# One hybrid encoder layer: attention's order written out for every engine, and the convolutions' middle stage interleaved

## The chip, the cores and the metric

The kernel runs on one core of a Trainium2 chip. A core has five engines with an instruction queue each: TensorE (PE, the matmul array, with a queue of its own for loading weights, PEld), VectorE (DVE), ScalarE (ACT), GpSimd (POOL) and SyncE (SP), which here only issues DMAs. Every queue is worked in its order; semaphores make an instruction wait for other engines and for DMAs. PE reads from SBUF and writes into PSUM, eight banks of 512 f32 columns; DVE and ACT read PSUM. The metric is the device time of one execution in microseconds.

## The reference

A layer has a token-mixing half and an expert half. The change is in the token mixing, of which this is the core (2048 tokens, 8 heads, 512 convolved channels):

```python
q = (rms_norm(cq_raw, q_norm_g) @ w_qb)                 # 8 heads x (64 + 32 rotary)
kv = (rms_norm(c_kv, kv_norm_g) @ w_kvb)                # keys and values of 8 heads
s = einsum('bqhd,bkhd->bhqk', qn, k_nope) + einsum('bqhr,bkr->bhqk', qr, k_rope)
p = softmax(s * scale, axis=-1)
a = einsum('bhqk,bkhd->bqhd', p, v)
...
z = parts[0]                                            # the other group: two long convolutions
for o in range(2):
    y = irfft(rfft(z, n=2 * S, axis=1) * filt_f[:, o], n=2 * S, axis=1)[:, :S]
    z = parts[o + 1] * (y + z * hyena_bias[o])
mixed = concatenate([rms_norm(a), rms_norm(z)]) @ w_o
```

## The kernel before, in words

The stage of the change lies between the input projection and the output projection. It has two streams of work that share all engines.

**Attention** (`attention`, lines 771 to 897) goes over 32 blocks: 8 heads, each with four blocks of 512 queries. A block has 16 steps over 128 keys. In a step PE makes the scores in three matmuls (lines 866 to 868, operands split into a high and a low part), ACT takes the exponential twice (lines 874 and 875, once rounded to the high part), DVE subtracts to get the low part (line 876, recorded at the helper's line 65), POOL adds the high part to an accumulator for the row sums (line 881), and PE multiplies with the values two steps later (`pv`, lines 859 and 860). The maximum of every row is found ahead, one block early, by `max_step`: one matmul (line 803) and one DVE reduction (line 805), 16 to a block. `max_row` turns the maxima into one more row of the query operand: DVE reduces and copies (lines 810, 811), PE transposes (814), ACT writes the row (815), and the next block's first score matmul reads it. `query` makes the query operand two blocks ahead; `free_sums` and `close_block` take a finished block out of PSUM, divide and store it. PSUM holds three score banks, two for maxima and the like (`x`), one each for the two value products, and one (`h`) for the other stream.

**The convolutions** (`hyena`, lines 631 to 768) are FFTs written as matmuls, for two orders `o` and two halves `i` of the channels: `spectrum` transforms the filters (matmul at line 669), `fwd1` is the first stage of the input's transform (652), `first_half` its second stage and the product with the spectrum (matmul 691, DVE 695, ACT 697 and 698, POOL 704 and 706), `second_half` the inverse's first stage (716), `inv` its last with the gate (736, 739). First and second half are the middle stage. All stages pass their results through DRAM (`Ad`, `F_dr`, `Bd`, `Z1`, `HY`), with loads and stores on SP's queue. Keys and values of the other heads (`values`, `other_keys`) come first in the same stream.

The two streams are generators. `drive` advances attention by a step and the other stream by a share of a step (1.5 for the first 12, then 0.7), and drains it at the end. This is only the order in which the code is written: the planner (`schedule_with_timeline_sim`) simulates the program with durations of its own and puts each engine's instructions in the order in which they come up there. Behind the stage, the output projection (lines 970 and on) loads `w_o` in eight pieces, splits each into a high and a low part (lines 1018, 1025), loads rows of both streams, transposes and multiplies (lines 73 to 75). Its weights are loaded into SBUF that the convolutions had.

Of the kernel before, what the change touches and what calls it, by code (L numbers as in the profile page):

```python
# [25 lines left out]
NT = 16  # L26
# [22 lines left out]
def hybrid_layer(ctx, tc, I, out):  # L49
# [581 lines left out]
    def hyena(hp, hw, bk):  # L631
# [7 lines left out]

        def fwd1(o, i, q4):  # L640
            hc = slice(i * HC, (i + 1) * HC)
            w1c = hw.tile([128, 4, 256], F32, name="ta", bufs=3)
            SY.dma_start(w1c, I["k_w1c"][:, q4 * 1024:q4 * 1024 + 1024].rearrange("p (q m) -> p q m", q=4))
            zt = hw.tile([128, 4, HC], F32, name="tb")
            SY.dma_start(zt, ZS[o][:, q4 * 4:q4 * 4 + 4, hc])
            for q2 in range(2):
                ev = hw.tile([128, 2, 2, HC], F32, name="tc")
                for qq in range(2):
                    ql = q2 * 2 + qq
                    p = bk("h")  # L650
                    for mt in range(2):
                        T.matmul(p[:, mt * HC:(mt + 1) * HC], w1c[:, ql, mt * 128:mt * 128 + 128], zt[:, ql, :],
                                 start=True, stop=True)
                    A.activation(ev[:, :, qq, :], p.rearrange("p (m c) -> p m c", m=2), AF.Copy)
                    if qq == 0:
                        yield
                for mt in range(2):
                    q0 = q4 * 4 + q2 * 2
                    SY.dma_start(Ad[2 * o + i][mt * 128:mt * 128 + 128, q0:q0 + 2, :], ev[:, mt])
                yield  # L660

        def spectrum(o, g4):
            kt = hw.tile([128, 4, CH], F32, name="tc")
            SY.dma_start(kt, pat(Af[o], g4 * 4 * 128 * CH, [[CH, 128], [128 * CH, 4], [1, CH]]))
            for g2 in range(2):
                ev = hw.tile([128, 2, CH], F32, name="ta", bufs=3)
                for gg in range(2):
                    p = bk("h")
                    T.matmul(p, g2m[:, 1 if g4 + g2 + gg == 0 else 0, :], kt[:, g2 * 2 + gg, :], start=True, stop=True)  # L669
                    A.activation(ev[:, gg, :], p, AF.Copy)  # L670
                    if gg == 0:
                        yield
                g0 = g4 * 4 + g2 * 2
                SY.dma_start(F_dr[o][g0:g0 + 2].rearrange("g p c -> p g c"), ev)
                yield

        def first_half(o, i, g4):
            hc = slice(i * HC, (i + 1) * HC)
            kt = hw.tile([128, 4, HC], F32, name="ta", bufs=3)
            SY.dma_start(kt, pat(Ad[2 * o + i], g4 * 4 * 128 * HC, [[HC, 128], [128 * HC, 4], [1, HC]]))  # L680
            ff = hw.tile([128, 4, 2, HC], F32, name="tc")
            for hh in range(2):
                SY.dma_start(ff[hh * 64:hh * 64 + 64], pat(F_dr[o], g4 * 4 * 128 * CH + i * HC,
                                                           [[CH, 64], [128 * CH, 4], [64 * CH, 2], [1, HC]]))
            ys = YS[g4] = []
            for g2 in range(2):
                gs = slice(g2 * 2, g2 * 2 + 2)
                p = bk("h")
                for gg in range(2):
                    gi = g2 * 2 + gg  # L690
                    T.matmul(p[:, gg * HC:(gg + 1) * HC], zm[:, 2 if g4 + gi == 0 else 0, :], kt[:, gi, :],
                             start=True, stop=True)
                pv = p.rearrange("p (g c) -> p g c", g=2)
                pr = hw.tile([128, 2, HC], F32, name="pr")
                V.tensor_tensor(pr, pv, ff[:, gs, 0], OP.mult)
                zs = hw.tile([128, 2, HC], F32, name="zs")
                A.activation(zs[0:64], pv[64:128], AF.Copy, scale=-1.0)
                A.activation(zs[64:128], pv[0:64], AF.Copy)
                yield
                if g4 + g2 == 0:  # L700
                    p = bk("h")
                    T.matmul(p[:, 0:HC], zm[:, 3, :], kt[:, 0, :], start=True, stop=True)
                    A.activation(zs[:, 0], p[:, 0:HC], AF.Copy)
                G.tensor_tensor(zs, zs, ff[:, gs, 1], OP.mult)
                y = hw.tile([128, 2, HC], F32, name="y", bufs=4)
                G.tensor_tensor(y, pr, zs, OP.add)
                ys += [y[:, 0], y[:, 1]]

        def second_half(o, i, g4):
            bt = hw.tile([128, 4, HC], F32, name="tb")  # L710
            ys = YS.pop(g4)
            for g2 in range(2):
                pi = bk("h")
                for gg in range(2):
                    gi = g2 * 2 + gg
                    T.matmul(pi[:, gg * HC:(gg + 1) * HC], ivm[:, 1 if g4 == 0 and gi == 0 else 0, :], ys[gi],  # L716
                             start=True, stop=True)
                A.activation(bt[:, g2 * 2:g2 * 2 + 2, :], pi.rearrange("p (g c) -> p g c", g=2), AF.Copy)
                yield
            SY.dma_start(pat(Bd[2 * o + i], g4 * 4 * 128 * HC, [[HC, 128], [128 * HC, 4], [1, HC]]), bt)  # L720

        def inv(o, i, q4):
# [4 lines left out]
            gt = hw.tile([128, 4, HC], F32, name="tb")  # L727
            SY.dma_start(gt, HZ[1 + o][:, qs, hc])
            for q2 in range(2):
                b2 = hw.tile([128, 2, 2, HC], F32, name="tc")  # L730
                q0 = q4 * 4 + q2 * 2
                SY.dma_start(b2, Bd[2 * o + i][:, q0:q0 + 2, :].rearrange("(k p) q c -> p k q c", k=2))
                p = bk("h")
                for qq in range(2):
                    for kt in range(2):
                        T.matmul(p[:, qq * HC:(qq + 1) * HC], w2i[:, q2 * 2 + qq, kt, :], b2[:, kt, qq, :],
                                 start=kt == 0, stop=kt == 1)
                q_ = slice(q2 * 2, q2 * 2 + 2)
                V.tensor_tensor(gt[:, q_], p.rearrange("p (q c) -> p q c", q=2), gt[:, q_], OP.mult)
                if q2 == 0:  # L740
                    yield
            SY.dma_start(ZO[o][:, qs, hc], gt)

        YS = {}

        def turns(*gens):
            gens = list(gens)
            while gens:
                for g in list(gens):
                    if next(g, gens) is gens:  # L750
                        gens.remove(g)
                    else:
                        yield

        for o in range(2):
            for g4 in range(8):
                yield from spectrum(o, g4)
            for i in range(2):
                for q4 in range(4):
                    yield from fwd1(o, i, q4)  # L760
            for i in range(2):
                yield from first_half(o, i, 0)
                for g4 in range(1, 9):
                    yield from turns(second_half(o, i, g4 - 1), *([first_half(o, i, g4)] if g4 < 8 else []))
            for i in range(2):
                for q4 in range(4):
                    yield from inv(o, i, q4)
                    yield


    def attention(kp, aw, bk):
        mz = kp.tile([128, 4, 128], F32, name="mz")
# [34 lines left out]
        def max_row(n):  # L807
            qh, ql, mx = blk[n]
# [16 lines left out]
        def close_block(n, osb, acc):  # L825
# [4 lines left out]
            for i in range(4):  # L830
# [5 lines left out]
                            rc[:, :, None].to_broadcast([128, 4, 64]), OP.mult)  # L836
            (G if n == NB - 1 else SY).dma_start(AO[:, b * 4:b * 4 + 4, h * 64:h * 64 + 64], oo)
# [4 lines left out]
        for j in range(16):  # L842
            max_step(0, j)
            yield
        max_row(0)
        pend = osb = None
        for n in range(NB):
            h, b = divmod(n, 4)
            if b == 0 and 0 < h < H - 1:
                load_head(h + 1)  # L850
            qh, ql, _ = blk[n]
            kh, kl, vt = khs[h % 2][:, 0], khs[h % 2][:, 1], vts[h % 2]
            po, pl = bk("o"), bk("l")
            acc = aw.tile([128, 512], F32, name="acc")
            ph = {}

            def pv(k):
                eh, el = ph.pop(k)
                T.matmul(po, vt[:, k, 0:128], eh, start=k == 0, stop=k == NT - 1)  # L859
                T.matmul(pl[0:66], vt[:, k, 64:130], el, start=k == 0, stop=k == NT - 1)  # L860

            maxes = iter(range(16))
            for k in range(NT):
# [11 lines left out]
                A.activation(p, p, AF.Exp, scale=SCALE)  # L875
                lo_of(V, el, p, eh)
                ph[k] = eh, el
# [4 lines left out]
                if k == 1 and pend is not None:  # L882
                    osb = free_sums(*pend[1:])
                if k >= 2:
# [811 lines left out]
```

## Time and profile before

| | |
|---|---|
| time, median of 3 runs | 3461.23 us (3448.82 to 3462.97) |
| the profiled execution | 3456.35 us, span 3454.6 us |
| PE busy over the span | 3196.6 us (93%) |
| DVE, ACT, POOL busy | 2301.5, 1697.8, 1456.5 us |

Busy counts the instructions' own time, and matmuls overlap each other. [...] In the chain of waits each entry is the time by which that instruction moved the end on, so that matmuls following each other without a gap show their pace there.

### The profile page before, as it was taken

Reading aid. Unit: us, or ns where it says so; the run is one execution under the profiler, and the core shown is the slowest. Engines: PE = TensorE matmul, PEld = TensorE weight load, DVE = VectorE, ACT = ScalarE, POOL = GpSimd, SP = SyncE. Lnnn points to the kernel's source line nnn. Section 1 sums busy time; section 2 is a strip of 40 time slices with the busy share of each in tenths; the row PEclk is TensorE's granted clock in tenths of the full one; section 3 lists DMA queues with packets and bytes.
Section 4 is the critical chain, followed back from the end, with each engine's and each line's share of the span. In section 5 each row is a group of like instructions: output and inputs, shape, how many; then the busy total and the mean of one; then the engine's idle time right before and its main releaser. Section 6 shows DMA issues by size and latency. Waiting matters only on the chain.

```text
span 3454.6 us, 41964 instructions
## 1 busy us (share of the span) xinstructions
PE 3196.6 (93%) x14790; PEld 2477.7 (72%) x14790; DVE 2301.5 (67%) x3528; ACT 1697.8 (49%) x2569; POOL 1456.5 (42%) x1134
## 2 busy tenths in 40 slices
PE   7899999899989999999998699599999999999897
PEld 3667787666767776677776488477788877887676
DVE  7975343776677776667774377776656566565886
ACT  4762222566667664667774244233444344444442
POOL 5750000556678784658886266300100010000564
PEclk9999999699999999999999899799999999999998
DMA  6444353356466467647456643455666566665784
GB/s 192 158 150 118 111 145 94 97 175 175 156 162 150 108 160 236 176 165 163 119 126 194 222 155 131 150 171 186 215 199 203 183 217 210 208 203 186 268 279 160
DMA packets 373755, 594.16 MB, mean 172 GB/s; under 512 B 36859, under 2 KB 190013, under 8 KB 373097
## 3 DMA queue, kind: packets, MB, share of 16 engines
q1 hardware_dynamic: 347097, 528.95, 48.5%
q0 software_dynamic: 26304, 62.00, 7.1%
q8 instruction: 117, 1.92, 0.2%
q14 instruction: 93, 0.76, 0.1%
q10 hardware_dynamic: 144, 0.52, 0.0%
HBM read 438.84 MB, written 152.58 MB: 171 GB/s over the span
## 4 chain that ended last, share of the span: by engine, by line
PE 70%; DVE 11%; DMA 8%; issue 4%; POOL 3%; ACT 3%; SPq 0%; POOLq 0%; DVEq 0%; ACTq 0%
PE g L73 9%; PE g L74 9%; PE g L75 8%; PE s L866 3%; PE s L867 3%; PE s L868 3%; PE o L859 3%; PE l L860 3%; PE x L803 3%; PE mm L75 3%; PE mm L74 3%; PE mm L73 3%; DMA w<-in_w_ada_dram 3%; PE h L669 2%; PE h L716 1%
## 5 line engine op out<-in xcount | busy, mean ns | idle before, releaser
L881 POOL TENSOR_TENSOR acc<-acc,eh 128x512 f32<-128x512 f32 x480 | 615.8, 1283 | 157.3 <-ACT eh L874 132.3
L65 DVE TENSOR_TENSOR wl<-raw,wh 128x2048 fp32r<-128x2048 f32 (+1 forms) x210 | 473.3, 2256 | 225.0 <-ACT wh L59 224.0
L59 ACT ACTIVATE wh<-raw 128x2048 fp32r<-128x2048 f32 x192 | 367.5, 1915 | 439.9 <-PE g L75 341.4
L65 DVE TENSOR_TENSOR el<-s,eh 128x512 fp32r<-128x512 f32 x512 | 349.2, 687 | 158.2 <-ACT s L875 153.2
L805 DVE TENSOR_REDUCE mx<-x 128x1 f32<-128x512 f32 x512 | 346.4, 685 | 140.5 <-PE x L803 138.1
L73 PE MATMUL g<-wh,xh 128*128 128x512 f32 x1024 | 411.1, 402 | 3.2 <-DVE xh L62 2.3
L74 PE MATMUL g<-wl,xh 128*128 128x512 f32 x1024 | 408.3, 399 | 1.6 <-DVE wl L65 1.5
L75 PE MATMUL g<-wh,xl 128*128 128x512 f32 x1024 | 407.5, 398 | 1.0 <-DVE xl L65 1.0
L874 ACT ACTIVATE eh<-s 128x512 fp32r<-128x512 f32 x512 | 304.9, 596 | 205.1 <-PE s L868 179.0
L1495 POOL DMA_INDIRECT ACC<-ye,idx x30 | 65.8, 2195 | 691.0 <-DVE ye L1486 565.5
L875 ACT ACTIVATE s<-s 128x512 f32<-128x512 f32 x512 | 304.5, 595 | 0.0
L860 PE MATMUL l<-el,vt 128*66 128x512 f32 x512 | 226.5, 446 | 0.6 <-DVE acc L820 0.4
L73 PEld LDWEIGHTS g<-wh,xh 128*128 128x128 f32 x1024 | 193.0, 188 | 47.0 <-DVE xh L62 3.1
L74 PEld LDWEIGHTS g<-wl,xh 128*128 128x128 f32 x1024 | 193.1, 189 | 45.4 <-DVE wl L65 2.7
L75 PEld LDWEIGHTS g<-wh,xl 128*128 128x128 f32 x1024 | 192.7, 188 | 45.7 <-DVE xl L65 1.8
L803 PE MATMUL x<-kh,qt 96*128 96x512 f32 x512 | 221.9, 446 | 1.8 <-DVE mx L805 1.6
L866 PE MATMUL s<-qt,kh 97*128 97x512 f32 x512 | 214.9, 420 | 3.3 <-ACT qt L815 2.7
L73 PE MATMUL mm<-uT,wh 128*128 128x512 f32 x512 | 207.8, 407 | 5.4 <-DVE uT L62 5.4
L73 PE MATMUL g<-wh,hh 128*128 128x512 f32 x512 | 205.9, 403 | 5.8 <-ACT hh L59 5.8
L74 PE MATMUL g<-wl,hh 128*128 128x512 f32 x512 | 205.9, 402 | 5.2 <-DVE wl L65 5.2
L867 PE MATMUL s<-qt,kh 96*128 96x512 f32 x512 | 208.2, 407 | 0.0
L868 PE MATMUL s<-qt,kh 96*128 96x512 f32 x512 | 207.2, 405 | 0.0
(408 smaller groups left out, 6988.9 us busy)
## 6 DMA issues: line engine op xcount, KB each, us to landing
raw<-in_w_gate_dram SPq DMA_DIRECT2D x64, 1024.0 KB, 5.0
raw<-in_w_up_dram SPq DMA_DIRECT2D x64, 1024.0 KB, 7.1
raw<-in_w_down_dram SPq DMA_DIRECT2D x64, 1024.0 KB, 10.1
tc<-F_dr SPq DMA_DIRECT2D x64, 512.0 KB, 5.2
w<-in_w_ada_dram SPq DMA_DIRECT2D x48, 512.0 KB, 4.4
Af<-ev SPq DMA_DIRECT2D x32, 512.0 KB, 2.6
tc<-Af SPq DMA_DIRECT2D x16, 1024.0 KB, 6.4
F_dr<-ta SPq DMA_DIRECT2D x32, 512.0 KB, 3.0
```

The costliest lines, as they stand in the source:

```text
L59: return A.activation(hi, src, AF.Copy)
L65: return eng.tensor_tensor(lo, src, hi.bitcast(F32), OP.subtract)
L73: first = T.matmul(o, wh, xh, start=start, stop=False)
L74: T.matmul(o, wh, xl, start=False, stop=False)
L75: T.matmul(o, wl, xh, start=False, stop=stop)
L803: T.matmul(p, qh[0:96, i * 128:i * 128 + 128], khs[h % 2][0:96, 0, c * 512:c * 512 + 512], start=True, stop=True)
L805: V.tensor_reduce(mx[:, i, c:c + 1], p, axis=AX.X, op=OP.max)
L860: T.matmul(pl[0:66], vt[:, k, 64:130], el, start=k == 0, stop=k == NT - 1)
L866: T.matmul(p, kh[0:97, ks], qh[0:97, :], start=True, stop=False)
L867: T.matmul(p, kh[0:96, ks], ql[0:96, :], start=False, stop=False)
L868: T.matmul(p, kl[0:96, ks], qh[0:96, :], start=False, stop=True)
L881: G.tensor_tensor(acc, acc, eh.bitcast(F32), OP.add)
```

## The change

The convolutions: `first_half` and `second_half` become one task, `mid`, whose step `g4` also does the second half of step `g4 - 1`. Each task first issues its loads, then computes in four steps; a fixed list of tasks interleaves the middle stage of one half with other stages of the other half. A task's loads are issued one task ahead, its stores one task behind. `fwd1` stores once for four columns, `inv` loads once. The tiles `tb` get three buffers, they had two.

Attention: the maxima are finished at step 12, `max_row` is done there, and its transposes and ACT's write, now `set_row`, at step 14. The last two value steps of a block are done in the first two steps of the next one. Steps 5 and 9 give the other stream no credit; the share is 0.8. `mz` is 98 columns wide, it was 128.

The order: all instructions of the stage are chained on their engine, each behind the one written before it, DMA issues too, with edges that order only and wait for nothing.

```diff
+        def mid(o, i, g4):
...
+            if g4 < 8:
+                kt = hw.tile([128, 4, HC], F32, name="ta", bufs=3)
...
+                ff = hw.tile([128, 4, 2, HC], F32, name="tc")
...
+            yield
+            done = YS.pop((i, g4 - 1), None)
...
+            for g2 in range(2):
+                if g4 < 8:
...
+                    yield
+                if done:
+                    pi = bk("h")
...
+                    yield
+            if done:
+                stores.append((pat(Bd[2 * o + i], (g4 - 1) * 4 * 128 * HC, [[HC, 128], [128 * HC, 4], [1, HC]]), bt))
...
+        def spread(mids, others, lead):
+            mids, others = list(mids), list(others)
+            for k in range(lead):
+                yield mids[k]
+            n = len(mids) - lead
+            for k in range(n - 1):
+                yield from others[k * len(others) // (n - 1):(k + 1) * len(others) // (n - 1)]
+                yield mids[lead + k]
+            yield mids[-1]
...
+        tasks = [*group(fwd1, 0, 0), *group(spectrum, 0),
+                 *spread(group(mid, 0, 0, n=nine), group(spectrum, 0, n=range(4, 8)) + group(fwd1, 0, 1), 1),
+                 *spread(group(mid, 0, 1, n=nine), group(inv, 0, 0) + group(fwd1, 1, 0) + group(spectrum, 1), 2),
+                 *spread(group(mid, 1, 0, n=nine), group(spectrum, 1, n=range(4, 8)) + group(inv, 0, 1)
+                         + group(fwd1, 1, 1), 2),
+                 *spread(group(mid, 1, 1, n=nine), group(inv, 1, 0, n=range(2)), 2),
+                 *group(inv, 1, 0, n=range(2, 4)), *group(inv, 1, 1)]
+        next(tasks[0])
+        for n, t in enumerate(tasks):
+            late, stores[:] = list(stores), []
+            for k, _ in enumerate(t):
+                if k == 0:
+                    for d, src in late:
+                        SY.dma_start(d, src)
+                    if n + 1 < len(tasks):
+                        next(tasks[n + 1])
+                yield
...
+        def set_row(n):
+            qh = blk[n][0]
             p = bk("x")
             for i in range(4):
-                T.transpose(p[:, i * 128:i * 128 + 128], mz[:, i, :], ident)
+                T.transpose(p[0:98, i * 128:i * 128 + 128], mz[:, i, :], ident)
             A.activation(qh[96:97, :], p[96:97, :], AF.Copy)
...
-                if n + 1 < NB:
-                    for j in itertools.islice(maxes, 2 if k in (7, 10) else 1):
-                        max_step(n + 1, j)
...
+                for j in itertools.islice(maxes, 2 if k in (2, 6, 11) else 1):
+                    max_step(n + 1, j)
                 lo_of(V, el, p, eh)
...
+                for g in {0: (-2,), 1: (-1,), 2: (), 3: (0,), 4: (1, 2)}.get(k, (k - 2,)):
+                    if g >= 0 or n > 0:
+                        pv(n + g // 16, g % 16)
+                if n > 0:
+                    if k == 1:
+                        done[n - 1] = free_sums(*live.pop(n - 1), accs[n - 1])
+                    if k == 5:
+                        oo = close_block(n - 1, done.pop(n - 1), accs.pop(n - 1))
+                    if k == 7:
+                        keep(n - 1, oo)
+                if k == 3 and b == 0 and 0 < h < H - 1:
+                    load_head(h + 1)
                 if k == 9 and n + 2 < NB:
                     query(n + 2)
-                if k == 14 and n + 1 < NB:
-                    max_row(n + 1)
-                yield
...
+                if n + 1 < NB:
+                    if k == 12:
+                        max_row(n + 1)
+                    if k == 14:
+                        set_row(n + 1)
+                yield k not in (5, 9)
...
-        drive(itertools.islice(at, 12), hy, 1.5)
-        drive(at, hy, 0.7, -1.0)
+        body = nc.cur_bb.bb.instructions
+        start, credit = len(body), 0.0
+        for n, free in enumerate(at):
+            credit += free * (1.5 if n < 12 else 0.8)
+            while credit >= 1.0:
+                credit -= 1.0
+                next(hy, None)
         drive(hy)
+        behind = {}
+        for ins in body[start:]:
+            e = ins.engine
+            if e in behind:
+                tc.add_manual_dep(ins, behind[e], mybir.DependencyInfo(mybir.DependencyClass.NoSync,
+                                                                       mybir.DependencyReason.DATA),
+                                  reason="the order written here")
+            behind[e] = ins.name
```

## Rows read from the trace of the kernel before

**Rows 1.** The page's first part: busy us, share of the span, instructions.
```profile
PE 3196.6 (93%) x14790; PEld 2477.7 (72%) x14790; DVE 2301.5 (67%) x3528; ACT 1697.8 (49%) x2569; POOL 1456.5 (42%) x1134
```

**Rows 2.** Busy by stretch: length, engines in Rows 1's order, granted clock, DMA share, GB/s.
```profile
661.00:1872.00 1211.00, 1139.98 (x4863) 867.66 (x4862) 868.13 (x1393) 809.94 (x1504) 880.20 (x718) 0.97 0.57 157
1870.00:1957.00 87.00, 42.29 (x144) 30.51 (x145) 18.53 (x29) 8.78 (x13) 4.97 (x7) 0.76 0.84 287
...
1870.00:1957.00 87.00, 34.81 (x104) 24.22 (x104) 0.76 0.84 287
...
1140.00:1165.00 25.00, 19.89 (x84) 15.58 (x84) 18.29 (x27) 13.35 (x25) 18.00 (x15) 0.86 0.58 132
```

**Rows 3.** The chain of waits inside attention: start us, us, what.
```profile
763.81 0.86 PE h L669 x2
...
902.49 0.23 PE s L866
...
907.14 0.86 PE h L652 x4
...
1150.25 1.71 PE h L691 x4
...
1233.85 0.79 PE x L829 x8
...
1863.60 1.73 PE h L736 x8
```

**Rows 4.** Groups of PE's matmuls, 640 to 1957 us: count, busy us, mean ns, idle before.
```profile
L860 PE MATMUL l<-el,vt 128*66 128x512 f32 x512 | 226.5, 446 | 0.6 <-DVE acc L820 0.4 <-DVE el L65 0.2
...
L736 PE MATMUL h<-tc,ta 128*128 128x256 f32 x256 | 72.3, 432 | 30.4 <-DMA tc<-Bd 18.1 <-DVE tb L739 10.7 <-DVE mx L805 1.6
...
L669 PE MATMUL h<-tc,g2m 128*128 128x512 f32 x128 | 68.1, 613 | 8.0 <-ACT ta L670 5.3 <-DMA tc<-Af 2.6
```

**Rows 5.** Lines 814 and 811: who waited for whom (us, times); ns min/median/max.
```profile
  DVE mz L811: 67.2, 35
...
L811 DVE COPY mz<-nm x32: 152/208/4784, 656.8 to 1838.9; 128x4 f32<-128x4 f32 x32
```

**Rows 6.** A block's end in time order: start us, us, engine, line, instruction.
```profile
1144.92 1.27 POOL L704 TENSOR_TENSOR zs<-zs,tc 128x512 f32<-128x512 f32 x1
...
1147.36 1.27 POOL L706 TENSOR_TENSOR y<-pr,zs 128x512 f32<-128x512 f32 x1
...
1145.09 3.57 DVE L811 COPY mz<-nm 128x4 f32<-128x4 f32 x1
...
1148.71 1.11 PE L814 MATMUL x<-ident,mz 128*128 128x128 f32 x4 [3.16 <-DVE mz L811]
```

**Rows 7.** Groups of the other engines, 640 to 2000 us, columns as in Rows 4.
```profile
L881 POOL TENSOR_TENSOR acc<-acc,eh 128x512 f32<-128x512 f32 x480 | 615.8, 1283 | 157.3 <-ACT eh L874 132.3 <-DVE qf L347 6.3 <-POOL acc L881 0.4
...
L805 DVE TENSOR_REDUCE mx<-x 128x1 f32<-128x512 f32 x511 | 345.7, 685 | 140.5 <-PE x L803 138.1
L874 ACT ACTIVATE eh<-s 128x512 fp32r<-128x512 f32 x512 | 304.9, 596 | 205.1 <-PE s L868 179.0 <-POOL acc L881 17.8 <-PE o L859 2.4
...
L697 ACT ACTIVATE zs<-h 64x512 f32<-64x512 f32 x64 | 38.1, 595 | 27.8 <-DVE pr L695 26.8
...
L346 DVE TENSOR_TENSOR osb<-x,CS 32x512 f32<-32x512 f32 x30 | 20.9, 696 | 5.9 <-PE x L75 5.3
...
L1025 DVE SCALAR_TENSOR_TENSOR wol<-raw,vcol,woh 128x1024 fp32r<-128x1024 f32 x7 | 8.7, 1282 | 8.7 <-ACT woh L1018 8.7
```

**Rows 8.** The chain of waits behind attention: start us, us, what.
```profile
1872.88 8.44 DMA tc<-Bd
...
1933.30 6.40 DMA raw<-in_w_o_dram
1939.72 9.75 DMA at<-AO
```

**Rows 9.** DMA issues, 640 to 1960 us: count, KB each, median us to landing.
```profile
tc<-Bd SPq DMA_DIRECT2D x32, 512.0 KB, 5.4
```

More of the change, by code (lines that the diff above doesn't have):

```diff
@@ L670, in spectrum @@
                     A.activation(ev[:, gg, :], p, AF.Copy)
-                    if gg == 0:
-                        yield
+                    yield
                 g0 = g4 * 4 + g2 * 2
-                SY.dma_start(F_dr[o][g0:g0 + 2].rearrange("g p c -> p g c"), ev)
-                yield
-        def first_half(o, i, g4):
+                stores.append((F_dr[o][g0:g0 + 2].rearrange("g p c -> p g c"), ev))
+        def mid(o, i, g4):
             hc = slice(i * HC, (i + 1) * HC)
[L679 to L685, printed above, removed]
-            for g2 in range(2):
[L687 to L700, printed above, removed]
-                    p = bk("h")
[L702 to L720, printed above, removed]
+            if g4 < 8:
+                kt = hw.tile([128, 4, HC], F32, name="ta", bufs=3)
+                SY.dma_start(kt, pat(Ad[2 * o + i], g4 * 4 * 128 * HC, [[HC, 128], [128 * HC, 4], [1, HC]]))
+                ff = hw.tile([128, 4, 2, HC], F32, name="tc")
+                for hh in range(2):
+                    SY.dma_start(ff[hh * 64:hh * 64 + 64], pat(F_dr[o], g4 * 4 * 128 * CH + i * HC,
+                                                               [[CH, 64], [128 * CH, 4], [64 * CH, 2], [1, HC]]))
@@ L722, in inv @@
+            if done:
+                stores.append((pat(Bd[2 * o + i], (g4 - 1) * 4 * 128 * HC, [[HC, 128], [128 * HC, 4], [1, HC]]), bt))
         def inv(o, i, q4):
@@ L742, in inv @@
[L742 to L768, printed above, removed]
+                yield
@@ new lines, in inv, with group @@
+            stores.append((ZO[o][:, qs, hc], gt))
+        YS, stores = {}, []
+        def spread(mids, others, lead):
[7 more added lines that the diff above has]
+            yield mids[-1]
+        def group(f, *a, n=range(4)):
+            return [f(*a, k) for k in n]
@@ L771, in attention @@
+        next(tasks[0])
[7 more added lines that the diff above has]
+                        next(tasks[n + 1])
+                yield
+        for d, src in stores:
+            SY.dma_start(d, src)
+        yield
     def attention(kp, aw, bk):
-        mz = kp.tile([128, 4, 128], F32, name="mz")
+        mz = kp.tile([128, 4, 98], F32, name="mz")
@@ L836, in close_block, with keep @@
                             rc[:, :, None].to_broadcast([128, 4, 64]), OP.mult)
+            return oo
+        def keep(n, oo):
+            h, b = divmod(n, 4)
             (G if n == NB - 1 else SY).dma_start(AO[:, b * 4:b * 4 + 4, h * 64:h * 64 + 64], oo)
@@ L843, in attention, with pv @@
             max_step(0, j)
-            yield
+            yield 1
         max_row(0)
-        pend = osb = None
+        set_row(0)
+        live, done = {}, {}
+        def pv(n, k):
+            if k == 0:
+                live[n] = bk("o"), bk("l")
+            po, pl = live[n]
+            eh, el = ph.pop((n, k))
+            vt = vts[n // 4 % 2]
+            T.matmul(po, vt[:, k, 0:128], eh, start=k == 0, stop=k == NT - 1)
+            T.matmul(pl[0:66], vt[:, k, 64:130], el, start=k == 0, stop=k == NT - 1)
+        ph, accs = {}, {}
         for n in range(NB):
             h, b = divmod(n, 4)
-            if b == 0 and 0 < h < H - 1:
-                load_head(h + 1)
             qh, ql, _ = blk[n]
[L852 to L862, printed above, removed]
+            kh, kl = khs[h % 2][:, 0], khs[h % 2][:, 1]
+            acc = accs[n] = aw.tile([128, 512], F32, name="acc")
+            maxes = iter(range(16 if n + 1 < NB else 0))
             for k in range(NT):
```

86 lines of the change are left out of this document (52 added, 34 removed).

## The prediction

> **What bounds the kernel now.** I read the page's first part, then the busy table by stretches, then the chain of waits inside attention, and last the groups by line. TensorE (PE) is the busy engine of the whole kernel [rows 1]. The change touches one stage only: from the first score matmul at 661 us to the last block's close at 1872 us, and the stretch behind it to 1957 us, where the output projection runs without gaps. In the first stretch (1211 us) PE is busy 1140 us at a mean granted clock of 0.97; ACT, DVE and POOL have 810 to 880 us of work. In the second (87 us) PE is busy 42 us at 0.76, and 35 of these are 104 records of the last convolution stage, line 736 [rows 2].
>
> Busy time overstates PE, because its matmuls overlap. The chain shows the pace when nothing waits: 0.23 us for a 512-column matmul of attention, 0.86 for one step of a convolution (two transforms, four records, or two records at 512 columns) [rows 3]. With the counts [rows 4] that gives PE's real work.
> - One block of attention: 16 steps of six matmuls (three scores, one for the maxima, two with the values) are 96 x 0.233 = 22.4 us; a query's six are 1.4; a close and the row of maxima, 8 matmuls and 8 transposes, are 1.6 at the 0.79 that eight take in the chain [rows 3]. That is 25.4 us, for 32 blocks 813; the first block's maxima and two queries lie ahead of 661 us, so 806.
> - The convolutions: lines 652, 691, 716 and 736 with 256 records each are 4 x 64 x 0.865 = 221; line 669 with 128 is 64 x 0.86 = 55; keys and values left at 661 us some 15, the rest 2. Together 293.
>
> So 1099 us at full clock. Of these the old kernel leaves 104/8 x 1.73 = 22 for the tail and does 1077 in 1211 us: 134 us lost, 4.2 a block. And it takes 85 us more from 1872 to 1957. These two are all the change can win.
>
> Where the 4.2 go is seen at a block's end. All of its values and maxima are done, and the next block's scores need the row of maxima: DVE copies it, PE transposes it, ACT writes it. PE's two queues wait 67 us for that copy in 35 places [rows 5]. [...] The tail is a chain of loads: a step waits 8.44 us for its input, the output weights are asked for only behind it (6.40 us), and behind them the rows of attention (9.75 us) [rows 8].
>
> **The change part by part.**
>
> *Order as written, on every engine.* A chain of order-only edges adds no instruction and no semaphore. It takes away what put the last transforms behind attention: by the written shares (18 steps, then 0.7 a step, for 318 steps) they should have been over in block 26, but the planner placed them last. Now 30 steps of keys and values and 321 of convolutions meet 18 + 3.2 credits ahead of the first block and 14 x 0.8 = 11.2 in each block, so they end in block 29 to 30. The tail's 22 us of PE move under attention; its 85 us become an end of about 10 us: the last block's sums, the close, and the split of the eight output weights, 1.28 us each on DVE [rows 7]. I take 10 (ends: 4, if the weights are split earlier; 30, if they are asked for as late as now). The convolutions' buffers come free 2.5 blocks before the end, so the weights' loads can lie under those blocks; if that cover is gone, the 6.40 and 9.75 us of now return.
>
> *The row of maxima in two parts.* The copy moves to step 12, the transposes to step 14, and the maxima end at step 12 (16 steps' worth, two in steps 2, 6 and 11). The last two value steps go over into the next block. So PE has score and value matmuls where it stood. That removes most of the 4.2. Late next: DVE at steps 13 to 15, which has only one instruction a step there; the copy is covered by some 2.5 us.
>
> *Value steps moved, sums freed at step 1.* The banks of sums (one each) are read by ACT and three DVE instructions, each like line 346's 0.70 us, 2.1 together [rows 7]. They now stand in DVE's order between step 1's remainder and step 2's two reductions. In a step PE has 0.7 us of scores, 0.23 of maxima, 0.47 of values and, in four steps of five, 0.86 of convolution; ACT's two exponentials (0.6 each) start 1.0 after the first score (three paces and the rest of the last one's 0.4), DVE's remainder and reduction are 0.69 each [rows 7]. So counted, step 1 ends on DVE at 5.1 us from the block's start, the sums at 7.2; PE gets to step 3's maximum at 7.25 and needs the first of step 2's reductions, at 7.9. So PE loses 0.7, or 1.0 where a product of the convolutions stands ahead.
>
> *The query at step 9, as written.* ACT's copy of the query waits for POOL's sum (1.28, as line 881's), that for two DVE products (0.70 each) [rows 7]. They start at 3.0 us after the step's first score, DVE ends at 4.4, POOL at 5.7, ACT at 6.4. The next exponential was ready at 3.8 and stands behind: 2.6 us late. PE runs on until it needs the one bank of the convolutions (6.7) or the maxima's banks (7.4); both come at 8.2 to 9.0. It loses 1.6 to 1.9 in 30 blocks. No row of before shows this: there the planner put ACT's copy after later exponentials. Ends: 0, if PE's lead holds; 4.4, if two POOL products of the middle stage (1.28 each) stand ahead. I take 1.8, the nearest to the rows.
>
> *The middle stage, spread.* Each pair holds its bank for two half-height copies of 0.595 on ACT [rows 7], 1.3 us with the release, against PE's 1.4 to the next use; I take 0.3 a block for lateness. POOL has 16 x 1.28 + 2.6 = 23.1 us a block; with the middle stage at one task in two, 30 of the block's 35: no bound. Only the last half has it nearly alone (37 against 35): about 7 us in all, inside the 0.3.
>
> *Loads a task ahead, stores a task behind, bigger pieces.* The same bytes in fewer instructions: 84 tasks of four steps. A load is asked for four steps before its use, 4/11.2 of 38 us = 13.5, and 512 KB land in 5.4 us [rows 9]; a task has up to 2 MB, and a store ahead of it in SP's queue, so 8 to 11 us. Late by nothing, then; with the cover gone it costs what it is late by, and PE now waits in order with attention behind.
>
> *Sum.* 0.8 + 1.8 + 0.3 is 2.9, less little overlaps 2.8 a block, 90 us (ends: 0, and 5.4 a block = 173). 661 + 1099 + 90 + 10 = 1860, where it was 1957: 97 us less. Profiled execution 3456.35 (span 3454.6) less 97 is 3359. That execution lies 4.9 below the median of the runs shown; I name 3360 and leave the 5 in the range.
>
> [...] The copy of the row took 0.21 us at the median but 4.78 at most [rows 5]; at 1145 it took 3.57, ending with the last of three POOL instructions that ran without a gap (the first and the last of them in [rows 6]). [...] POOL stays as full, so the change can't count on short copies; with the cover of step 13 to 15 it costs nothing, without it 2.8 x 32 = 90 us, all of the gain.
>
> **The rivals.**
> - *Nearly gapless*: ACT's and DVE's lags are absorbed by the three score banks, 1.0 lost a block. 661 + 1099 + 32 + 10 = 1802, so 3301. For it: free stretches of before run at the pace of [rows 3]. Against: one bank for the convolutions.
> - *Only the tail goes*: the written order loses as much as the planner's, 4.2. 1905, so 3404. For it: the old order also came from known durations; against: the wait of [rows 5] has no place left.
> - *ACT behind POOL*: at every query two middle products stand in POOL's queue ahead of its sum, 5.4 a block. 1943, so 3442. For it: POOL's 880 of 1211 us [rows 2]; against: the spread, and steps 5 and 9 give no credit.
> - *Slower, loads late*: PE waits in order for a task's input, and with it every score. Each of 84 tasks late by 2 us is 168: 3527. It decides from 97/84 = 1.2 us on. For it: the 8.44 us wait [rows 8]; against: 13.5 us of lead.
> - *It doesn't do what it says*: if the steps don't fit, a tail stays; each block too few adds 11 steps of 0.86 us, and the drain's loads. This lies between the second and the third, and its chance is in theirs.
>
> **How the numbers follow.** Forecast 0.44, gapless 0.19, only the tail 0.12, ACT behind POOL 0.17, loads late 0.08. The forecast's own range is 3330 to 3395. Reaching into the others until about 0.2 is left out: 3300 to 3435. A measurement tells 0.5% (17 us) from no change: faster 0.83 (the first three and half of the fourth), same 0.09, slower 0.08.
>
> **What would show it.** After: no record of line 736's successor behind the last close; PE's wait for the row of maxima gone; ACT's idle before the exponentials after a query, about 2.6 us, and PE waiting for a convolution bank there; the granted clock in the stage at 0.98 or more. Wrong if PE's waits for loads exceed 100 us, or if the stage between 661 and the output projection shrinks by less than 50 or more than 160 us.

## The result, and the profile after

The changed kernel takes 3564.48 us (median of 4 runs, 3562.74 to 3571.33), the kernel before 3455.22 beside it: a ratio of 1.0319, 95% interval 1.0288 to 1.035. It is slower by 109 us; 3360 was forecast, so the forecast missed by 204 us and had the sign wrong.

TensorE's share fell although it issues the same 14790 matmuls; its busy time rose by 40 us over [rows 1]. Most of that is clock: the granted clock (by the profile, a share of TensorE's full speed) was 0.958 in the whole execution before and is 0.947 now, an estimated 134 and 172 us of the busy time (0.042 of 3196.6 and 0.053 of 3236.9). The page's first part, after:

```profile
PE 3236.9 (91%) x14790; PEld 2497.1 (70%) x14790; DVE 2300.6 (64%) x3528; ACT 1711.1 (48%) x2569; POOL 1461.7 (41%) x1134
```

Busy time by stretch of the kernel after (columns as in [rows 2]): ahead of the first score, from there to the last block's close, and from there to the output projection's steady run:

```profile
640.00:700.50 60.50, 38.38 (x75) 21.06 (x75) 21.91 (x36) 18.78 (x38) 2.75 (x2) 0.50 0.37 127
...
700.50:2066.30 1365.80, 1192.85 (x4931) 897.90 (x4931) 870.39 (x1395) 814.21 (x1484) 884.47 (x720) 0.94 0.56 152
2066.30:2074.30 8.00, 6.43 (x26) 4.84 (x26) 5.75 (x11) 5.83 (x7) 0.87 (x2) 0.70 0.38 115
```

The tail of 85 us [rows 2] is gone: 8 us lie between the last close and the projection. But the first score comes at 700.5 us instead of 661, and the blocks take 1365.8 us. By the prediction's count of 1099 us of work, less some 9 us of matmuls that now lie ahead of the first score, that is 275 lost, 8.6 a block; the kernel before lost 4.2, and 2.8 was forecast. The output projection runs steadily from 2074 instead of 1957: these 117 us are the whole difference (the spans are 3569.6 and 3454.6).

What was waited for in the kernel after, 640 to 2070 us (us in total, times, longest), first TensorE's rows, then other engines':

```profile
PE h L715 <- ACT zs L701: 71.2, 45, 4.3
PE x L815 <- DVE mx L817: 42.9, 41, 2.3
...
PE h L652 <- DMA tb<-HZ: 8.3, 1, 8.3
...
PE h L736 <- DMA tc<-Bd: 2.8, 1, 2.8
...
PE x L829 <- DVE mz L823: 1.7, 1, 1.7
...
ACT zs L700 <- DVE pr L698: 125.9, 64, 4.1
...
ACT qf L803 <- DVE qf L347: 69.8, 29, 2.4
...
ACT qt L59 <- POOL qf L348: 24.2, 30, 1.4
...
PEld x L829 <- DVE mz L823: 2.6, 2, 2.4
```

The wait for the row of maxima is nearly gone: 1.7 us for the matmuls and 2.6 for the weight loads. The 67.2 us of [rows 5] are the sum of the same two queues, 29.9 and 37.3. Loads cost 11 us in two places. New is the first row: TensorE at line 715, the closing matmul of the middle stage, in front of ScalarE's copies (lines 700 and 701), and these in front of VectorE's product (line 698). In [rows 7] the same copies waited 26.8 us for that product; here it is 125.9. One such place in order of time (start us, us, engine, line, instruction, idle before):

```profile
907.22 1.02 PE L694 MATMUL h<-ta,zm 128*128 128x256 f32 x4
...
907.89 0.58 PE L887 MATMUL s<-qt,kh 97*128 97x512 f32 x1
908.13 0.69 DVE L65 TENSOR_TENSOR el<-s,eh 128x512 fp32r<-128x512 f32 x1 [1.84 <-ACT s L893]
...
908.74 0.68 DVE L698 TENSOR_TENSOR pr<-h,tc 128x512 f32<-128x512 f32 x1
...
909.24 0.40 PE L875 MATMUL l<-el,vt 128*66 128x512 f32 x1
909.33 0.68 DVE L817 TENSOR_REDUCE mx<-x 128x1 f32<-128x512 f32 x1
909.45 0.59 ACT L700 ACTIVATE zs<-h 64x512 f32<-64x512 f32 x1 [1.35 <-DVE pr L698]
910.05 0.59 ACT L701 ACTIVATE zs<-h 64x512 f32<-64x512 f32 x1
910.67 0.60 ACT L892 ACTIVATE eh<-s 128x512 fp32r<-128x512 f32 x1
910.70 1.13 PE L715 MATMUL h<-y,ivm 128*128 128x256 f32 x4 [1.06 <-ACT zs L701]
```

TensorE fills the bank `h` until 908.24. The product stands behind VectorE's remainder `el` and runs at 908.74, the copies follow one after the other until 910.64, and only then may line 715 write the bank: 2.46 us. TensorE had one attention step to put there, was done at 909.64, and stood 1.06 us with the next scores queued behind line 715. The next exponential stood behind the copies too. That is a ring through PE, DVE and ACT, closed by one bank.

Ahead of the first score, the same bank with the steps of keys and values (columns as above):

```profile
649.40 0.80 PE L73 MATMUL h<-wk,ckv 128*128 128x512 f32 x1 [1.41 <-DVE vv L65]
...
651.09 0.60 ACT L59 ACTIVATE vv<-h 128x512 fp32r<-128x512 f32 x1 [2.46 <-PE h L75]
651.72 0.69 DVE L65 TENSOR_TENSOR vv<-h,vv 128x512 fp32r<-128x512 f32 x1 [2.37 <-ACT vv L59]
...
652.46 0.80 PE L73 MATMUL h<-wk,ckv 128*128 128x512 f32 x1 [0.98 <-DVE vv L65]
```

One step takes 3.06 us, at a granted clock of 0.50 from 640 to 700.5 us. 19 such steps (57 of 84 matmul records) run ahead of the first score, where the planner had put 7 (21 records).

### The profile page after: what moved, and what is told of

It reads as the page before. It is cut to its first block, busy times and chain, and to the rows that moved or that the text cites. A ratio compares the mean times of both kernels' runs of the same rounds, so it can differ in the third digit from the quotient of the medians.

```text
span 3569.6 us, 41735 instructions
## 1 busy us (share of the span) xinstructions
PE 3236.9 (91%) x14790; PEld 2497.1 (70%) x14790; DVE 2300.6 (64%) x3528; ACT 1711.1 (48%) x2569; POOL 1461.7 (41%) x1134
## 4 chain that ended last, share of the span: by engine, by line
PE 64%; DVE 14%; ACT 7%; issue 5%; DMA 5%; POOL 4%; SPq 0%; POOLq 0%; ACTq 0%; DVEq 0%
PE g L73 9%; PE g L74 9%; PE g L75 9%; PE mm L75 3%; PE mm L74 3%; PE mm L73 3%; PE s L887 2%; PE o L874 2%; PE l L875 2%; DMA w<-in_w_ada_dram 2%; PE s L888 2%; PE x L815 2%; PE s L889 2%; PE h L715 2%; ACT eh L892 2%
## 5 line engine op out<-in xcount | busy, mean ns | idle before, releaser
L887 PE MATMUL s<-qt,kh 97*128 97x512 f32 x512 | 294.5, 575 | 0.7 <-ACT qt L830 0.7
L815 PE MATMUL x<-kh,qt 96*128 96x512 f32 x512 | 203.3, 426 | 47.2 <-DVE mx L817 42.9
L874 PE MATMUL o<-eh,vt 128*128 128x512 f32 x512 | 209.0, 408 | 2.3 <-DVE osb L837 2.3
```

Source lines behind the costliest of these rows:

```text
L887: T.matmul(p, kh[0:97, ks], qh[0:97, :], start=True, stop=False)
```

## The experiments

The theories, as the expectations name them. A: each badly placed instruction in the written order has a share of its own, ScalarE's first. O: the written order costs as such, wherever its instructions stand. S: the new structure of stages costs. D: what is saved at one wait is lost at the next. B: the cost is the ring through the one bank. F: a fixed order has a price even when well written. T: what the new structure gains is the tail. The kernel before stood between 3447 and 3457 us in the four groups of runs, so differences across groups are good to some 10 us. "The order" below is the chain of edges that fixes it.

**Without the order** (the planner places the new structure).

```diff
-            if e in behind:
-                tc.add_manual_dep(ins, behind[e], ...)
```

> The changed kernel without the chain of order-only edges: the same code, tasks and shares, but the planner orders each engine again. Theory A (ACT's queue: in the written order ACT waits, with the exponentials behind it, 64 times for DVE's product in the middle stage, 126 us of its idle time, and 30 times for DVE and POOL at a query, 94 us): the planner moves those copies, so most of the 115 us of slowdown go, and the tail is back or not; 3400 to 3470 us. Theory S (the new structure is what costs: tasks of four steps, middle stage interleaved): still 3530 to 3580.

Measured 3401.91 us, ratio 0.9849 (0.9828 to 0.987). The order costs 162 us and the structure gains 50: S falls. The same waits, as in the kernel after, from this kernel:

```profile
PE h L715 <- ACT zs L701: 10.5, 6, 2.2
...
ACT zs L700 <- DVE pr L698: 31.1, 35, 2.3
```

TensorE waits at line 715 in 6 places instead of 45; that the planner put other matmuls there is the likely reading. It did not end the tail: 56 records of the last convolution stage come behind the last close, where the kernel before had 96. The last close comes 18 us earlier than before (1855 against 1873) and the output projection's first transpose 49 us earlier (1901 against 1950), so 31 of its gain are a shorter tail.

**The order alone, in the kernel before.** The same edges, added to the old stages.

> The kernel before with the chain alone: its own code and shares, each engine in the order written. Theory O (a written order on every engine costs by itself, wherever the code was not arranged for it): clearly slower than before, 3550 to 3750, since here loads are also written right ahead of their use. Theory S: the chain is harmless, 3400 to 3480. Theory A expects slower too, by the same two waits and the loads: 3520 or more.

4178.22 us, ratio 1.2092 (1.207 to 1.2114). TensorE's longest waits there up to 2200 us, in a stage that lasts until 2681:

```profile
PE h L669 <- DMA tc<-Af: 76.0, 15, 7.2
PE h L736 <- DMA tc<-Bd: 59.0, 9, 8.0
PE x L814 <- DVE mz L811: 46.9, 24, 3.2
```

Over the whole stage the loads at line 736 come first, with 116 us. Old loads stood just ahead of their use. So the change's new stages repair most of what its order would break: of 726 us, 162 are left. The early loads and the split row are a part of that (11 us of loads and 1.7 for the row are left); the runs don't take it apart.

**ScalarE's copies ahead of VectorE's product.**

```diff
-                    V.tensor_tensor(pr, pv, ff[:, gs, 0], OP.mult)
                     zs = hw.tile([128, 2, HC], F32, name="zs")
                     A.activation(zs[0:64], pv[64:128], AF.Copy, scale=-1.0)
                     A.activation(zs[64:128], pv[0:64], AF.Copy)
+                    V.tensor_tensor(pr, pv, ff[:, gs, 0], OP.mult)
```

> The changed kernel with ACT's two copies of the middle stage written ahead of DVE's product from the same bank; nothing else. Theory A: ACT's 126 us of waiting for that product go, PE's 71 us of waiting for the copies shrink to under 20, and 60 to 110 us of time are won: 3450 to 3505. Theory O (no single place, the written order as such): under 20 us, 3545 to 3565, because DVE now waits for ACT instead.

3512.04 us, ratio 1.0171 (1.0154 to 1.0189): 52 less, between the two theories' numbers. The copies no longer wait; the bank still does, now for the product:

```profile
PE h L715 <- DVE pr L701: 50.2, 50, 4.3
PE x L815 <- DVE mx L817: 38.9, 40, 2.3
```

**The order on all engines but ScalarE**, with `if e in behind and e != A.engine`.

> The changed kernel with the chain on every engine but ACT, whose order the planner chooses. Theory A: the waits in front of the exponentials go, in the middle stage and at the queries: 80 to 160 us won, 3400 to 3485. Theory O: ACT's order follows the others', under 30 us: 3535 to 3565.

3542.68 us, ratio 1.0256 (1.0235 to 1.0277): 22 less. A's number fails. ScalarE's waits at the query are gone from the list, but TensorE waits longer for the copies at line 715, 95.0 us instead of 71.2. ScalarE free to choose still copies behind VectorE's product, which VectorE's written order keeps behind `el`; that this is why is argued, not shown.

**The order on TensorE alone**, with `e in (T.engine,)`.

> The changed kernel with the chain on TensorE alone; the planner orders ACT, DVE, POOL and the DMAs. Theory A (the cost sits in the written order of ACT and DVE): near the kernel without a chain (3402 us), 3390 to 3440. Its rival (TensorE's written order is itself what waits, whatever the others do): 3490 to 3560.

3530.9 us, ratio 1.0238 (1.0221 to 1.0255). TensorE's order by itself carries some 130 of the 162 us:

```profile
PE h L715 <- ACT zs L701: 87.2, 47, 5.4
PE o L874 <- DVE osb L837: 28.3, 17, 3.5
```

**The query spread over steps 9, 10 and 11**, on top of the copies ahead.

```diff
             rope_rows(qf, tmp, p, CS, cols, 64)
+            yield
             A.activation(qf[0:64], p[0:64], AF.Copy)
+            yield
             qt = aw.tile([128, 2, 512], F32R, name="qt", bufs=3)
```

> The changed kernel with ACT's middle-stage copies first (as in e3_zs_first, 3512 us) and the query spread over three steps: matmuls, DVE's products and POOL's sum at step 9, ACT's copy out of PSUM at step 10, ACT's high part and POOL's low part at step 11, each behind the step's exponentials. Theory A (each place where ready work stands behind a waiting instruction costs its own share): ACT's 97 us of waiting at the query go and PE gains about 1.6 us in each of 30 blocks: 3450 to 3475. Theory D (the lost time moves to the next wait): under 15 us won, 3497 to 3515.

3455.01 us, ratio 1.0023 (1.0013 to 1.0033): 57 less than with the copies alone, 1.9 for each of 30 queries. A holds. The wait for the maxima falls from 38.9 to 22.6 us, so that part of it was the query's:

```profile
PE h L715 <- DVE pr L701: 43.7, 52, 2.2
PE x L817 <- DVE mx L819: 22.6, 23, 2.3
...
PE h L704 <- DVE pr L701: 10.7, 4, 3.6
```

**The share of convolution steps 0.8 from the start** (`credit += free * 0.8`, no 1.5 in the first 12 steps), in the kernel after.

> The changed kernel (3564 us) with a share of 0.8 from the start, where it was 1.5 for the first 12 steps: 13 steps of values lie ahead of the first block in place of 21. Theory A: the first score matmul comes about 8 x 3.06 = 24 us earlier than 700.5, and 8 steps of 0.86 come back later: 15 to 25 us won, 3538 to 3552. Theory D: no gain, or a tail at the end again, 3555 to 3575.

3567.09 us, ratio 1.0344 (1.0327 to 1.0361). The first score came 26 us earlier, at 674.5, and the last close's matmuls no earlier (2068 against 2065): D.

**Both edits, that share, and the double maxima at steps 4, 7 and 11** instead of 2, 6 and 11.

> The changed kernel, the chain on every engine, with four places mended: the middle stage's copies first, the query over three steps, a share of 0.8 from the start, and the double maxima at steps 4, 7 and 11 in place of 2, 6 and 11, so that DVE has one reduction less behind the freed sums. Theory A: the shares add up, 52 + 48 + 20 + 20 to 30: 3380 to 3440. Theory D: 3470 or more.

3453.53 us, ratio 1.0013 (1.0002 to 1.0025), where the two edits alone gave 3455. Both ranges missed; that the two small edits bring nothing while the ring stands is as D says.

**A step more between two middle instructions**, on top of both edits (an empty `yield` behind each product with the spectrum, share 0.95).

> The kernel with the copies ahead and the query spread (median 3455), with an empty step written after each middle step, so that TensorE's next convolution instruction stands one attention step further behind the one that filled the bank; the steps' share is 0.95 instead of 0.8, since there are more of them. Theory B (the one bank of the convolutions: it is released by two copies and a product later than the one attention step between two middle instructions): TensorE's wait at the closing matmul of the middle stage falls from 44 us to under 15 and the time to 3400 to 3430. Theory D (what is saved is lost at the next wait of the written order): 3445 or more, with the wait at another line.

3439.43 us, ratio 0.9963 (0.9949 to 0.9977). TensorE's wait at the closing matmul (here line 716) went from 43.7 us in 52 places to none among its sixteen largest, as B says, but only some 20 us of time came with it, between the two ranges. The largest:

```profile
PE x L818 <- DVE mx L820: 36.9, 36, 3.7
...
PE h L73 <- DVE vv L65: 17.5, 16, 1.4
PE h L704 <- DVE pr L701: 15.0, 4, 4.6
```

**Two banks for the convolutions**, on top of both edits; the scores get two instead of three.

```diff
-        at_ = Banks(st, "psT", s=3, x=2, o=1, l=1)
-        hb_ = Banks(st, "psH", h=1)
+        at_ = Banks(st, "psT", s=2, x=2, o=1, l=1)
+        hb_ = Banks(st, "psH", h=2)
```

> The kernel with the copies ahead and the query spread (3455), with two banks for the convolutions and two for the scores instead of one and three. Theory B: the wait at the middle stage's closing matmul falls from 44 us to under 10; the time to 3400 to 3430 if two banks of scores do as well as three, and to more than 3455 if ScalarE's release of the score banks then holds TensorE, which would show as waits of the scores for the exponentials of over 40 us. Theory D: 3445 or more without such waits at the scores.

3375.38 us, ratio 0.9774 (0.9753 to 0.9796): 80 less than with one bank, more than B asked. The wait at line 715 is not in the list any more, nor is that at line 704, together 54 us with one bank, and the score banks are not short:

```profile
PE x L817 <- DVE mx L819: 36.4, 30, 2.9
...
PE s L889 <- DVE el L65: 6.7, 15, 2.3
```

Not all of the 80 is the middle stage. The steps of keys and values use the same bank, and the first score comes at 671.9 us instead of 697.8: 26 us. From there to the last close, with the copies ahead, then the query spread too, then the second bank (columns as above; the kernel after has 1365.80):

```profile
700.50:2002.30 1301.80, 1162.38 (x4931) 877.36 (x4931) 868.20 (x1395) 817.12 (x1484) 884.92 (x720) 0.97 0.59 159
...
697.80:1951.50 1253.70, 1151.91 (x4931) 876.96 (x4931) 891.84 (x1395) 817.96 (x1484) 883.73 (x720) 0.97 0.60 165
...
671.90:1871.60 1199.70, 1137.55 (x4931) 872.79 (x4931) 888.32 (x1395) 811.50 (x1484) 883.67 (x719) 0.98 0.64 173
```

**Two banks alone**, in the kernel after.

> The kernel after (3564) with two banks for the convolutions and two for the scores, nothing else: ScalarE's copies still stand behind VectorE's product and the query is still written at one step. Theory B (the loss is that of a ring through one bank): most of the 189 us between the kernel after and the one with all three edits (3375) comes with this edit alone, 3390 to 3450, and TensorE's wait for ScalarE's copies at the closing matmul falls from 71 us to under 15. Theory A (each place in ScalarE's written queue costs its own share, the bank only the rest): the two edits brought 109 us and the bank 80, so 3470 to 3500.

3492.99 us, ratio 1.0105 (1.0081 to 1.0129). The bank alone gives 71, not most of the 189: A's number, and B as the only cause falls. Here too 29 us are the first score's (671.3). With the ring gone, what ScalarE and VectorE are behind shows at the two score banks:

```profile
PE s L887 <- DVE el L65: 64.9, 78, 2.9
...
ACT zs L700 <- DVE pr L698: 130.9, 63, 5.0
...
ACT qf L803 <- DVE qf L347: 71.8, 30, 2.4
```

**Both edits without the order**, one bank.

> The kernel with the copies ahead and the query spread, without the fixed order: the planner orders each engine. Theory O (with the planner at work the order as written hardly matters, so what the two edits brought was a mending of the fixed order): within 10 us of the kernel after without the fixed order, 3392 to 3412. Theory B (the two edits save time of their own, 3 us a block): 3370 to 3390.

3429.99 us, ratio 0.9935 (0.9915 to 0.9955). Both theories missed: under the planner the two edits cost 28 us. Why is not shown.

**Both edits and two banks without the order.**

> The kernel with two banks, copies ahead and spread query (3375) without the fixed order. Theory F (a fixed order has a price of its own on top of the places where it is badly written): 20 to 60 us faster, 3315 to 3355. Theory B (with the ring gone the written order costs nothing against the planner's): within 15 us, 3360 to 3390. Slower than 3400 would say that the fixed order, well written, beats the planner's, as it did with one bank and both edits only the other way round (3430 without it, 3455 with it).

3402.35 us, ratio 0.9835 (0.9809 to 0.9861). With the same banks and edits the written order (3375) beats the planner's by 27 us, 21 by the ratios. F falls.

**Two banks in the kernel before**, the planner's order.

> The kernel before (3452) with two banks for the convolutions and two for the scores, the planner's order. Theory B (the one bank hurts because the written order can't go round it): within 25 us of the kernel before, 3430 to 3475, since the planner puts other work in the gap. The rival (one bank was the limit of every order): 3350 to 3400.

3433.31 us, ratio 0.993 (0.9906 to 0.9955): 0.7% faster, within B's range. So one bank costs the planner's order little in all, where it costs the written one 71 to 80. How the planner does it this run can't say, for it places the work otherwise: the convolutions end at 1584 us, there is no tail, and the last close comes at 1928 instead of 1873.

**The attention part of the change alone**, old convolutions, no order.

> The kernel before with the attention part of the kernel after (query at step 9, row of maxima in two parts, sums freed at step 1, the narrow tile), its convolutions as before and no fixed order. The new structure without the fixed order stands at 3402, 50 us under the kernel before. If the gain is that of the tail (theory T: convolutions that end earlier, as the prediction's largest term said), this kernel keeps the old tail and stands at 3435 to 3460; if it is the blocks' (the row of maxima, 67 us of waits before), at 3385 to 3415 with the wait for the mz copy under 25 us.

3441.22 us, ratio 0.9967 (0.9954 to 0.9979): in T's range. Attention brings about 11 of the 50 us that the structure gains under the planner; TensorE's matmuls still waited 30.3 us for the copy of the row, 29.9 before. T is only in part right all the same, as the kernel without the order kept a tail and won 18 us ahead of it (above). The convolutions' part alone was not run.

**Two banks, both edits, the maxima at 4, 7 and 11 and the share 0.8.**

> The kernel with two banks, copies ahead and spread query (3375), with the double maxima at steps 4, 7 and 11 instead of 2, 6 and 11 and the share 0.8 from the start. Theory D (what is saved turns up at the next wait): within 10 us, as with one bank, where the same two edits brought 1.5. Theory A (every waiting place has its own share): TensorE's wait for VectorE's maxima, 36 us, falls under 15, and the time to 3345 to 3360.

3343.8 us, ratio 0.9675 (0.9652 to 0.9699): the fastest of all. The two small edits brought 1.5 us while the ring stood and bring 32 without it. Busy by stretch from the first score to the last close, then a middle step in order of time:

```profile
655.30:1836.30 1181.00, 1131.66 (x4958) 864.33 (x4958) 885.71 (x1404) 816.54 (x1499) 884.57 (x719) 0.99 0.66 179
```

```profile
901.20 1.02 PE L694 MATMUL h<-ta,zm 128*128 128x256 f32 x4
...
902.26 0.59 ACT L699 ACTIVATE zs<-h 64x512 f32<-64x512 f32 x1 [0.64 <-PE h L694]
...
902.86 0.59 ACT L700 ACTIVATE zs<-h 64x512 f32<-64x512 f32 x1
...
903.21 0.40 PE L877 MATMUL l<-el,vt 128*66 128x512 f32 x1
903.45 1.02 PE L715 MATMUL h<-y,ivm 128*128 128x256 f32 x4
...
903.49 0.69 DVE L701 TENSOR_TENSOR pr<-h,tc 128x512 f32<-128x512 f32 x1 [0.77 <-ACT zs L700]
```

Line 715 starts before the product has read the other bank, with no idle time ahead of it. TensorE is busy with nearly the same matmuls 1131.66 us at a granted clock of 0.99, where the kernel after took 1192.85 at 0.94: 61 of the 185 us between these two stretches. By the clocks, an estimated 0.06 of 1192.85 and 0.01 of 1131.66, the difference would be 60.

The two orders side by side, medians in us:

| kernel | planner's order | written order |
|---|---|---|
| before | 3452 | 4178 |
| as changed | 3402 | 3564 |
| copies ahead, query spread | 3430 | 3455 |
| and two banks | 3402 | 3375 |
| and maxima, share | not run | 3344 |

## Why the prediction was wrong

**The step that failed: "The middle stage, spread."** It read: "Each pair holds its bank for two half-height copies of 0.595 on ACT [rows 7], 1.3 us with the release, against PE's 1.4 to the next use; I take 0.3 a block for lateness." The pair also holds its bank for VectorE's product, and the copies wait for that: 2.46 us at 907 us, not 1.3. The row was in hand: in [rows 7] the copies' idle is 26.8 us behind that product; I took their mean and passed over their wait. Under the planner the wait was cheap: TensorE waited 3.9 us in 2 places at this line (716 there) for the copies. In TensorE's written order the scores stand behind it, and it waited 71.2 us in 45. Copies ahead (52 us, 64 in the profiled blocks) and the second bank's share in the blocks (54 us) measure 106 to 118 us, 3.3 to 3.7 a block against 0.3. That is the largest part of the 204 us.

In the traces the copies start behind the product (64 waits, 125.9 us, in the kernel after), and the product behind the copies where these were written ahead (40 waits, 38.2 us, in the kernel with two banks). Why the two readers of the bank come one behind the other is not shown.

**The start, left out.** The sum took 661 us for the first score as given. It came at 700.5. The share of 1.5 for the first 12 steps is not new, but the planner had not kept to it; the written order does, and it puts 19 steps of keys and values ahead of the first score instead of 7, at 3.06 us each. The prediction counted these credits ahead of the first block and did not charge them. What the 39 us are worth depends on what follows: starting 26 us earlier brought nothing in the kernel after, while the second bank shortened these steps by 26 to 29 us. Between the last two written kernels 17 us are the first score's (671.9 to 655.3), and 19 lie in the blocks.

**The query, right.** 1.8 in 30 blocks were forecast, 54 us; spreading it gave 57 (48 in the profiled blocks). ScalarE waits there nearly as described: the copy itself stands behind VectorE's second product (69.8 us in 29 places) and not behind POOL's sum, for which the next instruction waits (24.2 in 30). Together that is 3.1 us a query, 2.6 were forecast.

**Sums freed at step 1, about right.** 0.7 to 1.0 a block were forecast. Of the 42.9 us of waiting for the maxima 22.6 are left with the query spread, 0.7 a block, though 36.4 with the second bank. With the double maxima later 5.8 us are left in the last kernel; there TensorE waits 11.2 us for the sums themselves, 1.5 before that edit.

**The tail, the row of maxima, the loads: right.** 8 us for the tail (10 forecast), 67.2 to 4.3 us of waits for the row in both queues, and 11 us for loads. The rival that had the slower side, late loads at 3527, was wrong in its mechanism; slower came by another way. The long copies of [rows 5] had no place: the copy took 0.35 us at the median and 0.81 at most, under cover.

**The sum.** The projection runs steadily at 2074 instead of the forecast 1860, 214 us later: 39 at the first score, 177 in the blocks, 2 less in the tail. Added one after the other, the edits shorten the profiled blocks from 1365.8 us to 1301.8 (copies), 1253.7 (query), 1199.7 (second bank) and 1181.0 (maxima and share). So of the 275 lost, where 90 were forecast, 118 belong to the middle stage (10 forecast), 48 to the query (54), and some 28 to the sums and the maxima (26): 19, and 9 because the last kernel has that much more work behind its first score. The kernel with all edits still loses 1181 - 1099 = 82 us, 2.6 a block. The sum had no term for these, and no run takes them apart; 49 of them are TensorE's idle time. The shares hold in this order only: the bank gave 71 alone and 80 behind the other two edits, the small edits 1.5 or 32.

Of the signs that the prediction named, the granted clock in the stage came as 0.94 and not as 0.98 or more, and the stage did not shrink by 50 to 160 us. The kernel with all edits has 0.99, and its projection at 1844, 113 earlier than before.

## What to carry to other kernels

Before an order is fixed, count for each PSUM bank the whole round from the last matmul in to the next matmul in, with every engine that reads it and what stands ahead of each reader; compare it with what the in-order engine has to do in between. A wait that is cheap under a planner marks a place where a written order can stall, and it is no upper bound: the copies' 26.8 us became 125.9. Charge the round there and not the old wait. Count as well what the written order puts ahead of the first step. Try a small edit again once the larger wait is gone, as its gain can be hidden until then.

## What the runs showed of the hardware

Less idle time came with a higher granted clock: between first score and last close, with the same 4931 matmul records, TensorE stood idle for 173 us (stretch less busy time) and was busy 1192.85 us at a granted clock of 0.94 in the kernel after, 102 and 1151.91 at 0.97 with the copies ahead and the query spread, 62 and 1137.55 at 0.98 with the second bank too. And two score banks cost little where the copies and the query were well placed: TensorE waited for them 6.7 us with all three edits, and 64.9 us where the copies and the query stood as written.
